# A two-layer decoder trunk on one Trainium2 core: late stores on GpSimd's queue, the gate row written between the layers, biases in four transfers, score-bank fill on ScalarE, and the scale columns spread anew

## The chip, the cores and the metric

The kernel runs on one core of one Trainium2 chip (trn2). A core has five engines with a queue of instructions each: TensorE (PE in the profile; PEld is its weight load), VectorE (DVE), ScalarE (ACT), GpSimd (POOL) and SyncE (SP), which issues transfers. Every engine works through its queue in order, and waits on semaphores where it needs what another one makes. Transfers can be issued from SP, ACT and POOL, and run on 16 DMA engines.

The metric is the device time of one execution in microseconds (us), as the median of a few runs. A profiled execution has its own time, and a span from its first to its last instruction.

## The reference, cut to what matters

A sequence of 1024 rows of width 1024 goes through two layers. Layer 0 is a gated pooling mixer of width 2048; layer 1 is gated sliding-window attention (window 128, 16 query heads in 4 groups that the kernel takes one after another, 2 shared key/value heads) with a sink per head and a relative-position bias. Before each sub-layer stands RMSNorm with a shift and a scale worked out from a condition vector c, and behind it a gate from c.

```python
for l in range(DEPTH):                       # DEPTH = 2
    shift, scale, gate = split(silu(c) @ ada_w[l] + ada_b[l], 3)
    if l == 0:
        h = rmsnorm(x, norm_g[0]) * (1 + scale) + shift
        u, z = split(h @ w_in, 2)
        p = causal_multiscale_pool(u)        # trailing means over 2, 4, 8, 16 rows, minus u
        y = (einsum(p, w_group) * a_scale * silu(z)) @ w_out
    else:
        # one K/V from x, with its own norm, shift and scale
        kb, vb = shared_kv_blocks(x, silu(c), kv_norm_g, kv_ada_w, kv_ada_b, w_kv)
        h = rmsnorm(x, norm_g[1]) * (1 + scale) + shift
        q, z = split(h @ w_in, 2)
        s = q @ kb.T / 8 + pos_bias          # masked to the band of 128
        p = exp(s - m) / (sum(exp(s - m)) + exp(sink - m))
        y = ((p @ vb) * silu(z)) @ w_out
    x = x + gate * y
return rmsnorm(x, final_g)
```

## The kernel before, in words

**Tiling.** x is held transposed, as 8 tiles of 128 channels by 1024 rows, each worked on in two halves of 512 rows. Every fp32 operand is split into a high and a low part (`wh`, `wl` for a weight: ACT copies the high part, DVE subtracts for the low one), and each product is made of three matmuls: high by high, high by low, low by high. PE's order is that in which the code is written.

**Layer 0.** First the pooling stage (to about 420 us), then the output product in 16 *half products*: `order` lists pairs (n, hf) of an output tile n and a half hf of the 2048 inner channels; `out_half(i)` runs one. Tiles 0 to 4 (below `LATE = 5`) take both halves of the rows, 10.4 us each half product; tiles 5 to 7 take only the first half of the rows here and the second one in the next stage. The first six (`BESIDE = 6`) are written in a block in which only PE's order is by hand; in the ten that follow, all queues are in the order of the code.

**The scale columns.** The 64 columns of shift, scale and gate (48 for the two layers, 16 for K/V) are dot products, 128 at a time, of rows of `ada_w` and `kv_ada_w` with silu(c). 48 of them (`rest_cols`) are not wanted at once: for each, `ada_step` loads a 128x1024 tile into one of three `tmp` buffers from SP's queue, and one DVE instruction (`ada_dot`, L284) makes a column of `adac`. They are dealt out: 18 in the pooling stage, `ADA[i]` before the i-th of the first six half products, and the letters A in `JOBS` beside the last ten, where the load goes out from POOL's queue three jobs ahead (`ask`). A letter S there is another job: a weight of layer 1 is loaded, split and written back to DRAM (`stage_split`, `keep`). The last 8 columns are the gates of layer 1, `adac[:, 40:48]`.

**Between the layers** (about 556 to 605 us) a list of steps with times (`plan`, `at`) is sorted and written out for PE, ACT, DVE and POOL: the rest of the output product (`last_chunk`), the squares and the reciprocal root for the norm (`rstd_stats`), the modulation of two sets of eight tiles (`step_h`, `fold_l`), the loads of weights (`get_raw`) and their splits (`take_h`, `take_l`; L1057, L1061), and the shared K/V products. After it one transfer from ACT's queue loads the biases (L1105).

**Layer 1** is written as notes: each has an engine, a length, what it reads and writes. A planner (`in_order`) keeps PE's notes in their order and gives every other note a due time from those that need it; then it runs a clock over all queues, and takes on each the ready note that is due first. The lengths thus set only the order. `attend` is one block of 128 rows for four heads: scores into a bank of PSUM (`scores`), for block 0 with a memset of the missing part (L1413), then DVE takes the band out of it (L1422), adds the bias (L1429), ACT takes the exponential; the transposed probabilities are split, POOL selects parts of them (L1472) into `pp` and `ph`, two SP transfers copy half of `pp` to the other 64 partitions (L1483), and PE blends them with V (L1504, L1514). Weights of layer 1 that have been split once are kept in DRAM (`kw`), and fetched back from POOL's queue (L1758).

**The end.** For the last 128 rows, layer 1's gates and `final_g` are needed as rows: `rows_in` writes `adac[:, 40:48]` to DRAM as `row` from SP (L1635), and loads it and `fg_row` back to all partitions (L1641), the first after the write. `finish(0, 4, ...)` scales the first 512 rows and stores them, eight transfers of 256 KB from SP (`store`, L1858).

Of the kernel before, what the change touches and what calls it, by code (L numbers as in the profile page):

```python
# [18 lines left out]
P = 128  # L19
# [25 lines left out]

ADA = (0, 0, 2, 6, 8, 8)

BESIDE = 6

JOBS = ("S", "SA", "SA", "SA", "SA", "", "SA", "", "SA", "")  # L50

# [47 lines left out]
def trunk(ctx, tc, xT, c, pack, ada_first, ada_rest, wu0_in, wg0_in, wa, wg, wao, wkv,  # L99
# [48 lines left out]
    for i in range(16):  # L148
# [7 lines left out]
                            channel_multiplier=1, compare_op=ALU.is_ge, fill=0)  # L156

    early = cp.tile([P, 1], F32, name="early")
    nc.scalar.activation(early, ones, AF.Exp)
# [101 lines left out]
    with ExitStack() as sa:  # L261
# [610 lines left out]
        with tc.manual_schedule(engines={ET.PE}):  # L872
# [70 lines left out]
            def out_half(i):  # L943
# [7 lines left out]
                if hf == 1:  # L951
                    for q in qs:
                        residual(n, q, outs[n][q], 16)
                    for q in qs:
                        square_add(n, q)

            for i in range(BESIDE):
                ws[order[i + 1]] = half_w(*order[i + 1])
                if i == 0:
                    gather(8, 9)  # L960
                    new_x()
                    again_x(0)
# [9 lines left out]
        with tc.manual_schedule(engines={ET.PE, ET.Activation, ET.DVE, ET.Pool, ET.SP}):  # L972
            stage_hi = [slot("stage") for _ in range(2)]
            raw = fetch(wao[order[BESIDE + 1]])
            jobs, asked = list("".join(JOBS)), []
            for _ in range(3):
                ask()
            for i in range(BESIDE, len(order)):
                if i + 1 < len(order):
                    ws[order[i + 1]] = split_w(*raw)  # L980
                if i + 2 < len(order):
                    raw = fetch(wao[order[i + 2]])
                if i < KT:
# [5 lines left out]
            assert rest_at[0] == len(rest_cols) and not staged  # L989
            mod_scale(8, 56, C_KVG)  # L990
            mod_scale(16, 32, C_NG + 8)
# [84 lines left out]
        for i in range(nl):  # L1076
            at(NT * i, last_chunk, i)
            if i % 4 == 3:
                t, n = NT * (i + 1), late[i // 4]
                at(t + AFTER[0], lambda n: residual(n, 1, got[n], 16), n)  # L1080
                at(t + AFTER[1], square_s, n, 1)
                at(t + AFTER[2], square_a, n, 1)
        at(NT - 0.01, lambda: put("st", rstd_stats, sqh[0], 4))
        at(2 * NT - 0.01, lambda: nc.scalar.copy(out=rb, in_=rstd_spread(got["st"], 4)))
# [19 lines left out]
    bias = bp.tile([P, 16, P], F32, name="bias")  # L1104
    nc.scalar.dma_start(bias, bias_in)  # L1105
    KH = [bp.tile([P, T], F32R, name=f"KH{i}") for i in range(2)]
# [144 lines left out]
    X = [there(x) for x in xk]  # L1251
    KHb, KLb, VSb = [there(t) for t in KH], [there(t) for t in KL], there(VS)
    ring_of("wh", got["wv"][0], got["wq"][0])
    ring_of("wl", got["wv"][1], got["wq"][1])
# [136 lines left out]
    def attend(q, r, b):  # L1391
# [16 lines left out]
        def scores(j):  # L1408
# [3 lines left out]
            if b == 0:  # L1412
                note(DVE, 0.2, lambda: nc.vector.memset(s()[:, :, :P], NEG), (), [(bk, "off")])  # L1413

            def f():
                for e in range(2):
# [4 lines left out]
                 [(qt, (j, e, i, c)) for e in range(2) for i in range(2)] + k_on, [(bk, 0)])  # L1421
            note(DVE, 0.36, lambda: nc.vector.copy_predicated(  # L1422
                out=s()[:, :, :P], mask=tri, data=s()[:, :, P:]), [(bk, "off")], [(bk, 0)])
# [3 lines left out]
        def row(s, bk, e, i):  # L1427
# [38 lines left out]
        if b:  # L1466
# [4 lines left out]
            def some(to, h, sign, base):  # L1471
                note(POOL, 0.65, lambda: nc.gpsimd.affine_select(  # L1472
                    out=v8(to(), h), in_=v8(cur(), h).bitcast(F32),
                    pattern=[[0, 2], [0, 4], [-sign, 2], [-2 * sign, P // 4]], base=base,
                    channel_multiplier=sign, compare_op=ALU.is_ge, fill=0.0),
                    [(cur, (x, h)) for x in range(2)] if to is not cur else (),
                    [(to, (x, h)) for x in range(2)])
# [50 lines left out]
        def add(e):  # L1528
            es = slice(e * 2 * P, (e + 1) * 2 * P)
            note(DVE, 0.36, lambda: nc.vector.scalar_tensor_tensor(  # L1530
                out=of()[e * 64:(e + 1) * 64, :], in0=o()[0:64, es], scalar=0.5,
                in1=ol()[0:64, es], op0=ALU.mult, op1=ALU.add),
                [(o, 0), (o, 1), (ol, 0)], [(of, e)])
        for e in range(2):
            add(e)
        ofv = lambda: of().rearrange("p (j c) -> p j c", c=P)
        note(DVE, 0.5, lambda: nc.vector.tensor_mul(out=ofv(), in0=ofv(), in1=sz()[:, :, cols]),
             [(sz, 0), (sz, 1)], [(of, 0), (of, 1)])
# [36 lines left out]
    def out_part(q, part, n2):  # L1575

        def run(w):
            acts = heads(q, part, range(4))

            def tile(i, n):  # L1580
                def done(ps):
                    note(DVE, 0.68, lambda: residual(n, q, ps(), 40), [(ps, 0)], x_on(n, q))
                    if part == 1:
                        note_square(n, q)
# [46 lines left out]
    def rows_in():  # L1631

        row = kp.tile([KT, P], F32, name="row")
        at = there(row)
        note(SP, 0.35, lambda: nc.sync.dma_start(  # L1635
            row.rearrange("n p -> p n"), adac[:, 40:48]), last_w[3][0].on, [(at, 0)], 4.0)
# [131 lines left out]
    def split_any(key, raw, w):  # L1768
# [8 lines left out]
        else:  # L1777
# [3 lines left out]
        note(ACT, 1.0, lambda: nc.scalar.copy(out=w[0](), in_=raw()), [(raw, 0)], w[0].on)  # L1781
        note(DVE, 1.16, lambda: nc.vector.tensor_sub(
            out=w[1](), in0=raw(), in1=w[0]().bitcast(F32)), [(raw, 0)] + w[0].on, w[1].on)
# [45 lines left out]
    def finish(t0, n, gap):  # L1829
# [4 lines left out]
        def gen():  # L1834
# [46 lines left out]
    class Second:  # L1881
# [5 lines left out]
        def step(self, k):  # L1887
            if k % 2 == 0:
# [3 lines left out]
            b = adac[:, self.shift + k:self.shift + k + 1]  # L1892
            note(DVE, 0.77, lambda: nc.vector.scalar_tensor_tensor(
                out=f(), in0=xk[k][:, half(1)], scalar=a, in1=rb(), op0=ALU.mult, op1=ALU.mult),
# [172 lines left out]
```

## Time and profile before

| | |
|---|---|
| runs | 953.55, 954.9 and 952.06 us; median 953.55 |
| profiled execution | 956.07 us; its span 954.4 us |
| mean granted clock of TensorE | 0.989 |
| VectorE's work on the 48 scale columns | 60.7 us, and 37.6 us idle before them |
| DMA | 172.14 MB, 180 GB/s in the mean |

Of the profile's views, the list of waits tells for each engine what ended its idle time. A wait for several things is put down to the one that came last. In a group of instructions stand: line, engine, operation, out<-in, shapes, count, then busy us and mean ns of one, then idle us just before them with what ended it. A busy engine other than PE costs time only where PE waits for it.

### The profile page before, as it was taken

How to read it: one execution, taken by the hardware profiler on the slowest of the kernel's cores; microseconds unless marked ns; L12 is line 12 of the kernel's file. 1: busy time of each engine (PE TensorE's matmuls, PEld its weight loads, DVE VectorE, ACT ScalarE, POOL GpSimd, SP SyncE). 2: the span in 40 equal slices, each digit the busy share in tenths (PEclk: the TensorE clock that was granted, in tenths of full speed). 3: DMA queues.
4: the chain of work that ended last, by engine and by line, in shares of the span. 5: the costliest groups of instructions: out<-in, count | busy, mean ns of one | idle time of the engine just before them, and what ended most of it. 6: DMA issues, size and time to landing. Idle time of an engine off the chain costs nothing.

```text
span 954.4 us, 13163 instructions
## 1 busy us (share of the span) xinstructions
PE 917.1 (96%) x4532; PEld 800.4 (84%) x4532; DVE 761.8 (80%) x1382; ACT 493.0 (52%) x1000; POOL 175.4 (18%) x285
## 2 busy tenths in 40 slices
PE   8999899999999998999889999999999999998997
PEld 6887788888888887888778887788888888997887
DVE  6999989777997799786773759479999956776785
ACT  6546554433443354672122336377878656666544
POOL 3000000000000000000012200224324445545631
PEclk9999999999999999999999999999999999999999
DMA  9553441164216420778887933954776765567022
GB/s 342 185 181 111 141 168 66 52 236 155 67 50 237 154 67 23 264 229 308 289 290 272 324 117 132 346 164 156 251 259 214 236 189 184 161 206 180 18 101 89
DMA packets 61047, 172.14 MB, mean 180 GB/s; under 512 B 8498, under 2 KB 16818, under 8 KB 60851
## 3 DMA queue, kind: packets, MB, share of 16 engines
q1 hardware_dynamic: 48306, 125.14, 38.3%
q0 software_dynamic: 12240, 44.57, 14.3%
q10 hardware_dynamic: 432, 1.57, 0.5%
q8 instruction: 36, 0.59, 0.2%
q14 instruction: 33, 0.26, 0.1%
HBM read 129.04 MB, written 36.70 MB: 174 GB/s over the span
## 4 chain that ended last, share of the span: by engine, by line
PE 48%; DVE 30%; DMA 12%; issue 6%; ACT 4%; POOL 1%; DVEq 0%; ACTq 0%; POOLq 0%; SPq 0%
PE ps_d L1268 7%; PE ps_d L1266 7%; PE ps_d L1267 7%; PE ps_d L257 5%; DMA tmp<-ada_rest 5%; PE ps_d L695 4%; DVE tmp L593 4%; PE ps_S L257 4%; DVE ws L666 2%; PE ps_S L695 2%; PE ps_tp L257 2%; DVE ad L284 1%; DVE tw L670 1%; PE ps_tp L695 1%; DVE p L616 1%
## 5 line engine op out<-in xcount | busy, mean ns | idle before, releaser
L284 DVE CUSTOM_DVE_ANT_0 tmp<-tmp,cact,pk 128x1024 f32<-128x1024 f32 x48 | 60.7, 1281 | 37.6 <-DMA tmp<-ada_rest 37.5
L257 PE MATMUL ps_d<-gh,wh 128*128 128x512 f32 x224 | 80.5, 383 | 0.0
L695 PE MATMUL ps_d<-hs,ws 128*128 128x512 f32 x312 | 72.1, 380 | 1.4 <-ACT ws L665 1.0
L1433 ACT ACTIVATE P<-P,nm 128x129 f32<-128x129 f32 x128 | 50.2, 394 | 34.9 <-DVE nm L1429 34.5
L1266 PE MATMUL ps_d<-hm,wh 128*128 128x512 f32 x176 | 67.9, 386 | 0.0
L695 PEld LDWEIGHTS ps_d<-hs,ws 128*128 128x128 f32 x312 | 58.8, 189 | 10.7 <-ACT ws L665 1.4
L1268 PE MATMUL ps_d<-hm,wl 128*128 128x512 f32 x176 | 66.8, 379 | 0.0
L1267 PE MATMUL ps_d<-hm,wh 128*128 128x512 f32 x176 | 66.8, 379 | 0.0
L257 PE MATMUL ps_S<-gh,wh 128*128 128x512 f32 x192 | 65.2, 380 | 0.0
L665 ACT CAST ws<-tw 128x512 fp32r<-128x512 f32 x52 | 31.8, 620 | 59.9 <-DVE tw L670 30.7
L1472 POOL TENSOR_SCALAR_AFFINE_SELECT pp<-ph 128x512 fp32r<-128x512 f32 x56 | 48.5, 883 | 72.4 <-DVE ph L1462 31.7
L585 POOL MEMSET tmp<- 128x16 f32 x12 | 1.3, 111 | 327.1 <-DVE tmp L593 112.3
L695 PE MATMUL ps_d<-ha,ws 128*128 128x512 f32 x252 | 57.8, 379 | 0.0
L695 PEld LDWEIGHTS ps_d<-ha,ws 128*128 128x128 f32 x252 | 47.7, 189 | 6.7
L257 PEld LDWEIGHTS ps_d<-gh,wh 128*128 128x128 f32 x224 | 42.7, 191 | 6.1
L1472 POOL TENSOR_SCALAR_AFFINE_SELECT ph<-ph 128x512 fp32r<-128x512 f32 x56 | 46.3, 843 | 0.0
L593 DVE TENSOR_TENSOR tmp<-tmp 128x1039 f32<-128x1039 f32 (+3 forms) x36 | 44.4, 1233 | 1.0
L257 PE MATMUL ps_d<-gh,wl 128*128 128x512 f32 x112 | 42.8, 382 | 0.0
L1444 ACT ACTIVATE P<-P,den 128x128 f32<-128x128 f32 x128 | 40.6, 390 | 3.1 <-DVE den L1440 3.1
L257 PEld LDWEIGHTS ps_S<-gh,wh 128*128 128x128 f32 x192 | 36.2, 189 | 4.9
L170 ACT CAST wh<-raw 128x1024 fp32r<-128x1024 f32 x24 | 25.2, 1049 | 27.7 <-PE ps_d L257 24.0
L257 PE MATMUL ps_d<-p,wh 128*128 128x512 f32 x96 | 36.6, 381 | 2.4 <-ACT p L615 1.7
(350 smaller groups left out, 2684.3 us busy)
## 6 DMA issues: line engine op xcount, KB each, us to landing
tmp<-ada_rest SPq DMA_DIRECT2D x42, 512.0 KB, 4.8
raw<-wa SPq DMA_DIRECT2D x28, 512.0 KB, 3.3
raw<-wao SPq DMA_DIRECT2D x20, 512.0 KB, 5.8
raw<-kw POOLq DMA_DIRECT2D x20, 512.0 KB, 4.6
wh<-kw POOLq DMA_DIRECT2D x19, 512.0 KB, 3.6
wl<-kw POOLq DMA_DIRECT2D x19, 512.0 KB, 4.8
ad<-ada_first SPq DMA_DIRECT2D x16, 512.0 KB, 4.5
x<-xT SPq DMA_DIRECT2D x32, 256.0 KB, 5.8
```

Of the source, the lines that this page charges most:

```text
L170: nc.scalar.copy(out=wh, in_=raw)
L257: mm(p, lhs, acts(k, hl, q), start=start and k == ks[0] and s == 0, stop=stop and k == ks[-1] and s == 2)
L284: nc.vector.tensor_tensor_reduce(out=raw, in0=raw, in1=ca, scale=0.5, scalar=pk[:, bcol:bcol + 1], op0=ALU.mult, op1=ALU.add, accum_out=ad ...
L593: nc.vector.tensor_add(out=nx[:, 2 * s - 1:], in0=cur[:, 2 * s - 1:], in1=cur[:, s - 1:PAD + T - s])
L665: nc.scalar.copy(out=ws[i][:, 0, :], in_=src)
L695: mm(ps, lhs, acts(k, hl), start=start and k == 0 and s == 0, stop=k == 3 and s == 2, skip_group_check=True)
L1266: mm(p, lh, a[0](), start=k == 0, stop=False)
L1267: mm(p, lh, a[1](), start=False, stop=False)
L1268: mm(p, ll, a[0](), start=False, stop=k == n - 1)
L1433: note(ACT, 0.41, lambda: nc.scalar.activation(pt()[:, i, :P + 1], pt()[:, i, :P + 1], AF.Exp, bias=nm()[:, i:i + 1], scale=-1.0, accum_ou ...
L1444: note(ACT, 0.3, lambda: nc.scalar.activation(pt()[:, i, :P], pt()[:, i, :P], AF.Copy, scale=den()[:, i:i + 1]), [(den, i)], [(pt, i)])
L1472: note(POOL, 0.65, lambda: nc.gpsimd.affine_select(out=v8(to(), h), in_=v8(cur(), h).bitcast(F32), pattern=[[0, 2], [0, 4], [-sign, 2], [- ...
```

## The change

- `ADA` falls from 24 to 16 columns, and `JOBS` gets three more A, in the iterations that had no job. The five columns that are left (`n_late`) are put into the plan between the layers, at 0.4, 1.9, 3.4, 4.9 and 6.4 us of its time, and their loads go out from SP.
- Beside the first half products the next half weight is fetched one iteration ahead (`fetch`, then `split_w`).
- The write of `row` moves from the end into the plan between the layers, at 9.0, on ACT's queue. The loads of the two rows go from SP to ACT, both after the split of the last weights; the first no longer follows the write.
- The biases are loaded in four transfers of four heads each from SP, as notes, and the step that adds the bias reads its own part.
- The score bank's memset on DVE becomes a copy on ACT from a constant tile `off`, which POOL fills at the start.
- The eight stores of the first 512 rows go from SP to POOL.
- Lengths of some notes are raised (DVE's, and POOL's selects from 0.65 to 0.85).

```diff
-ADA = (0, 0, 2, 6, 8, 8)
+ADA = (0, 0, 2, 4, 5, 5)
...
-JOBS = ("S", "SA", "SA", "SA", "SA", "", "SA", "", "SA", "")
+JOBS = ("S", "SA", "SA", "SA", "SA", "A", "SA", "A", "SA", "A")
...
+    off = cp.tile([P, P], F32, name="off")
+    nc.gpsimd.memset(off, NEG)
...
+            raw = fetch(wao[order[1]])
             for i in range(BESIDE):
-                ws[order[i + 1]] = half_w(*order[i + 1])
+                ws[order[i + 1]] = split_w(*raw)
+                raw = fetch(wao[order[i + 2]])
...
-            raw = fetch(wao[order[BESIDE + 1]])
             jobs, asked = list("".join(JOBS)), []
...
+        row = kp.tile([KT, P], F32, name="row")
+        n_late = len(rest_cols) - rest_at[0]
+        for i in range(n_late):
+            at(0.4 + 1.5 * i, ada_step)
+        at(9.0, lambda: nc.scalar.dma_start(row.rearrange("n p -> p n"), adac[:, 40:48]))
         at(NT - 0.01, lambda: put("st", rstd_stats, sqh[0], 4))
...
-    nc.scalar.dma_start(bias, bias_in)
...
+    biasb = there(bias)
...
-                note(DVE, 0.2, lambda: nc.vector.memset(s()[:, :, :P], NEG), (), [(bk, "off")])
+                note(ACT, 0.36, lambda: nc.scalar.copy(
+                    out=s()[:, :, :P], in_=off.unsqueeze(1).broadcast_to([P, 2, P])),
+                    (), [(bk, "off")])
...
-            note(DVE, 0.36, lambda: nc.vector.copy_predicated(
+            note(DVE, 0.4, lambda: nc.vector.copy_predicated(
...
-                accum_out=nm()[:, i:i + 1]), [(bk, 0)], [(pt, i), (nm, i)])
+                accum_out=nm()[:, i:i + 1]), [(bk, 0), (biasb, hd // 4)], [(pt, i), (nm, i)])
...
-                note(POOL, 0.65, lambda: nc.gpsimd.affine_select(
+                note(POOL, 0.85, lambda: nc.gpsimd.affine_select(
...
     def rows_in():
 
-        row = kp.tile([KT, P], F32, name="row")
-        at = there(row)
-        note(SP, 0.35, lambda: nc.sync.dma_start(
-            row.rearrange("n p -> p n"), adac[:, 40:48]), last_w[3][0].on, [(at, 0)], 4.0)
         rows = (row.rearrange("n p -> (n p)").unsqueeze(0), fg_row)
 
-        def load(name, src, on):
+        def load(name, src):
             t = end[name] = tile_of("raw1", bp, [P, 1024], F32, 2)
-            note(SP, 0.35, lambda: nc.sync.dma_start(t(), src.broadcast_to([P, D])),
-                 on, [(t, 0)], 4.0)
-        load("gate", rows[0], [(at, 0)])
-        load("gain", rows[1], ())
+            note(ACT, 0.35, lambda: nc.scalar.dma_start(t(), src.broadcast_to([P, D])),
+                 last_w[3][0].on, [(t, 0)], 4.0)
+        load("gate", rows[0])
+        load("gain", rows[1])
...
             def store(k):
-                note(SP, 0.35, lambda: nc.sync.dma_start(outT[k * P:(k + 1) * P, ts], xk[k][:, ts]),
+                on, by = (POOL, nc.gpsimd) if n == 4 else (SP, nc.sync)
+                note(on, 0.55 if n == 4 else 0.35,
+                     lambda: by.dma_start(outT[k * P:(k + 1) * P, ts], xk[k][:, ts]),
                      x_of(k), (), 3.0)
...
+    def bias_part(r):
+        hs = slice(4 * r, 4 * r + 4)
+        note(SP, 0.35, lambda: nc.sync.dma_start(bias[:, hs], bias_in[:, hs]),
+             (), [(biasb, r)], 5.0)
+    for r in range(4):
+        bias_part(r)
```

The other lengths that change: the two additions of `add(e)` from 0.36 to 0.4, the gating product from 0.5 to 0.58, the residual from 0.68 to 0.72, the low part of a weight from 1.16 to 1.22, and the modulation's first step from 0.77 to 0.85.

More of the change, by code (lines that the diff above doesn't have):

```diff
@@ L988, in trunk @@
                 out_half(i)
-            assert rest_at[0] == len(rest_cols) and not staged
+            assert not staged
             mod_scale(8, 56, C_KVG)
@@ L1529, in add @@
             es = slice(e * 2 * P, (e + 1) * 2 * P)
-            note(DVE, 0.36, lambda: nc.vector.scalar_tensor_tensor(
+            note(DVE, 0.4, lambda: nc.vector.scalar_tensor_tensor(
                 out=of()[e * 64:(e + 1) * 64, :], in0=o()[0:64, es], scalar=0.5,
@@ L1536, in attend @@
         ofv = lambda: of().rearrange("p (j c) -> p j c", c=P)
-        note(DVE, 0.5, lambda: nc.vector.tensor_mul(out=ofv(), in0=ofv(), in1=sz()[:, :, cols]),
+        note(DVE, 0.58, lambda: nc.vector.tensor_mul(out=ofv(), in0=ofv(), in1=sz()[:, :, cols]),
              [(sz, 0), (sz, 1)], [(of, 0), (of, 1)])
@@ L1581, in done @@
                 def done(ps):
-                    note(DVE, 0.68, lambda: residual(n, q, ps(), 40), [(ps, 0)], x_on(n, q))
+                    note(DVE, 0.72, lambda: residual(n, q, ps(), 40), [(ps, 0)], x_on(n, q))
                     if part == 1:
@@ L1781, in split_any @@
         note(ACT, 1.0, lambda: nc.scalar.copy(out=w[0](), in_=raw()), [(raw, 0)], w[0].on)
-        note(DVE, 1.16, lambda: nc.vector.tensor_sub(
+        note(DVE, 1.22, lambda: nc.vector.tensor_sub(
             out=w[1](), in0=raw(), in1=w[0]().bitcast(F32)), [(raw, 0)] + w[0].on, w[1].on)
@@ L1892, in step @@
             b = adac[:, self.shift + k:self.shift + k + 1]
-            note(DVE, 0.77, lambda: nc.vector.scalar_tensor_tensor(
+            note(DVE, 0.85, lambda: nc.vector.scalar_tensor_tensor(
                 out=f(), in0=xk[k][:, half(1)], scalar=a, in1=rb(), op0=ALU.mult, op1=ALU.mult),
```

## The prediction

> **What bounds the kernel now.** I read the share of busy time by engine first, then the list of TensorE's (PE's) waits, then the stretches in which the longest waits lie (busy time, granted clock and DMA by stretch), and last the rows of the engine or queue that each wait names.
>
> ```profile
> PE 917.1 (96%) x4532; PEld 800.4 (84%) x4532; DVE 761.8 (80%) x1382; ACT 493.0 (52%) x1000; POOL 175.4 (18%) x285
> ```
>
> PE is busy for 917.1 of 954.4 us. Its order of work is fixed and the change adds no matmul, so what the change can win is a part of the 37.3 us in which PE stands, and what the clock loses after a stop. Here are PE's waits that the edits touch (total in us, times, longest):
>
> ```profile
> PE ps_o L1514 <- DMA pp<-pp: 4.5, 1, 4.5
> PE ps_o L257 <- DVE wl L172: 2.9, 2, 2.0
> PE ps_tp L257 <- DVE wl L172: 2.4, 2, 1.7
> PE ps_S L1418 <- DVE ps_S L1413: 2.2, 1, 2.2
> PE ps_d L1268 <- DMA raw<-kw: 1.7, 1, 1.7
> PE ps_d L246 <- DVE wl L1061: 1.1, 2, 0.6
> PE ps_o L1504 <- POOL ph L1472: 0.9, 2, 0.5
> ```
>
> And the stretches around them (length; busy time of each engine; then granted clock, DMA share, GB/s):
>
> ```profile
> core 0: us, PE busy (x) PEld busy (x) DVE busy (x) ACT busy (x) POOL busy (x), PEclk, DMA share, GB/s
> 481.50:487.00 5.50, 5.50 (x18) 4.54 (x19) 3.64 (x6) 0.00 (x0) 0.00 (x0) 0.69 0.90 311
> 564.10:602.00 37.90, 36.18 (x163) 30.26 (x162) 36.17 (x47) 23.50 (x26) 0.65 (x2) 1.00 0.40 141
> 692.70:698.50 5.80, 5.74 (x26) 5.16 (x27) 5.33 (x18) 4.72 (x16) 1.39 (x3) 0.71 0.83 272
> 864.40:874.00 9.60, 9.60 (x59) 8.71 (x58) 8.98 (x22) 6.31 (x19) 5.66 (x8) 1.00 0.47 33
> 874.00:882.00 8.00, 3.53 (x16) 3.09 (x15) 2.29 (x11) 2.44 (x10) 1.67 (x2) 0.78 1.06 355
> 882.00:888.00 6.00, 6.00 (x22) 4.91 (x22) 3.64 (x6) 2.89 (x8) 3.94 (x5) 0.72 0.13 40
> ```
>
> The reader is to see three things. A stop of PE of 2 us or more is paid twice: the stretch behind the 2.0 us stop has a clock of 0.69, which loses 5.5 x 0.31 = 1.7 us; behind the 2.2 us stop 5.8 x 0.29 = 1.7; around the 4.5 us stop 8 x 0.22 + 6 x 0.28 = 3.4. Between 564 and 602 us, which is the stretch between the layers, VectorE (DVE) is busy for 36.2 of 37.9 us and so has no room. And from 864.4 to 874 us the DMA engines are 0.47 busy but move only 33 GB/s.
>
> **The change, part by part.** *Scale columns before the layers' seam.* Each of the 48 columns is a load and one DVE instruction (L284). 24 of them lie in the six half products after the pooling stage (434 to 493 us):
>
> ```profile
> L284 DVE CUSTOM_DVE_ANT_0 tmp<-tmp,cact,pk 128x1024 f32<-128x1024 f32 x24 | 30.3, 1282 | 20.2 <-DMA tmp<-ada_rest 20.1
> L172 DVE TENSOR_TENSOR wl<-raw,wh 128x1024 fp32r<-128x1024 f32 x4 | 4.9, 1218 | 0.0
> ```
>
> DVE spends 30.3 us on them and 20.2 us standing before them for their loads, and the weight splits (L172), which PE waits for, stand behind them in DVE's order. That is 50.5 us for 24, or 2.1 us each. With 16 in their place DVE gets 8 x 2.1 = 17 us free in this stretch, against four waits of 2.9 + 2.4 = 5.3 us in all. So I take all of the 5.3 away, and the 1.7 us of clock behind the longest: 7.0 (bounds 3.5 and 7.0). That the half weights are asked for one earlier adds nothing by itself: DVE had 0.0 idle before L172, so their loads were not late. Three of the eight go to GpSimd's (POOL's) queue, into a stage for which the list of waits names nothing; they could bring back there what left here, so between 0 and 5.3; I take 0.5, nearer to the row that is absent.
>
> *Five columns between the layers.* They come ahead of the modulation of layer 1 in DVE's order, and the rest of DVE's work is queued behind them.
>
> ```profile
> 558.54 0.24 DVE L303 SCALAR_TENSOR_TENSOR acol<-adac,pk 128x8 f32<-128x8 f32 x2
> 559.86 0.16 DVE L208 TENSOR_SCALAR v<-ps_o 128x4 f32<-128x4 f32 x1 [1.08 <-PE ps_o L205]
> 564.11 0.75 DVE L1017 SCALAR_TENSOR_TENSOR tmp<-x,acol,rb 128x512 f32<-128x512 f32 x1 [4.09 <-ACT rb L1084]
> ...
> L284 DVE CUSTOM_DVE_ANT_0 tmp<-tmp,cact,pk 128x1024 f32<-128x1024 f32 x48 | 60.7, 1281 | 37.6 <-DMA tmp<-ada_rest 37.5
> ```
>
> Five times 60.7 / 48 = 1.26 is 6.3 us; DVE's idle time here is 1.08 + 4.09 = 5.2, so at best 1.1 us is left over, less 0.5 for two memsets of 0.27 that leave DVE (row below). But there are three buffers, and a load takes 4.8 us to land (row below): if the first column ends at 560.0, the fourth lands at 564.8, and the fifth ends near 567.4 instead of 564.1. From there to 602 DVE is full and PE already waits for its splits (L246, 1.1), so most of it reaches PE. If all five loads are late, it is 7. I take 3.0 (bounds 0.6 and 7).
>
> *The row of gates.* The trace shows what its write does:
>
> ```profile
> 862.04 0.58 SPq L1635 DMA_DIRECT2D row<-adac  x1
> 868.67 2.13 SPq L1483 DMA_DIRECT2D pp<-pp  x2
> ...
> tmp<-ada_rest SPq DMA_DIRECT2D x42, 512.0 KB, 4.8
> raw<-wao SPq DMA_DIRECT2D x20, 512.0 KB, 5.8
> pp<-pp SPq DMA_DIRECT2D x56, 64.0 KB, 1.9
> out<-x SPq DMA_DIRECT2D x8, 256.0 KB, 2.2
> bias<-bias_in ACTq DMA_DIRECT2D x1, 1024.0 KB, 9.1
> raw<-row SPq DMA_DIRECT2D x1, 512.0 KB, 8.8
> row<-adac SPq DMA_DIRECT2D x1, 4.0 KB, 11.7
> ...
> 868.67 11.52 DMA pp<-pp
> ```
>
> 4 KB, in pieces of 4 bytes, take 11.7 us from 862.04 to 873.7, which is the stretch at 33 GB/s; the copy of pp behind it takes 11.52 us (last row, from the chain of waits) instead of 1.9, and PE waits for it. With the write gone from here, the 4.5 and the 3.4 us go: 7.9 (bounds 4.5 and 7.9). Next late is the copy at its usual 1.9 us: it would land at 870.6, and PE came to it at 880.2 - 4.5 = 875.7. The write is now issued by ScalarE (ACT) between the layers, and drains there for 9.6 us. What it meets there are the loads of wao, and after them those of the K/V weights:
>
> ```profile
> 566.31 5.73 SPq L179 DMA_DIRECT2D raw<-wao  x2
> 576.12 1.03 ACT L1057 CAST wh<-raw 128x1024 fp32r<-128x1024 f32 x1
> ```
>
> The first is asked for at 566.31 and split from 576.12, 9.8 us later; it needs 5.8, so 4.0 are in hand. Caught whole by the drain it is 9.6 - 4.0 = 5.6 late, with 3.4 of clock behind it: bounds 0 and 9.0. I take 1.0, since it goes out before DVE has done the first tile's modulation, behind which ACT issues the write. The two broadcast loads of rows now go out from ACT when the last weights are split, without waiting for the write; ACT's exponentials stand behind the two issues. 0.
>
> *The score bank.* Eight memsets of 0.27 us leave DVE for ACT. One is late:
>
> ```profile
> 691.07 1.23 DVE L1782 TENSOR_TENSOR wl<-raw,wh 128x1024 fp32r<-128x1024 f32 x1
> 692.35 0.27 DVE L1413 MEMSET ps_S<- 128x256 f32 x1
> ```
>
> It stands behind a weight split, and costs PE 2.2 + 1.7 = 3.9. ACT is only 52% busy over the span, but busy in 4.72 of the 5.80 us after 692.7, so a fill there can be late as well: bounds 0 and 3.9, and I take 3.0.
>
> The Trainium skill (TensorE: Matmul & The Clock Gate, Part 1: The HAM clock gate) has the clock halved after an idle window of about 3.4 us. By that, stops of 2.0 and 2.2 us cost no clock, and their two 1.7 us are not there to win: 943.1 in the end (rival 5). The rows of 0.69 and 0.71 behind just these stops disagree, and I go by them.
>
> *The biases.* One transfer of 1 MB on ACT's queue (9.1 us) becomes four on SyncE's (SP's), with the same bytes. PE's 1.7 us wait for a kept weight at 609 us falls into it. The four parts start a little later, and only the first is wanted soon; the scores of each head group now wait for their part. Bounds -1.7 (the same wait once more) and 1.7; I take 1.0 off.
>
> *The stores.* Eight stores go from SP to POOL, whose instructions of this kind are
>
> ```profile
> L1758 POOL DMA_DIRECT2D raw<-kw x20 | 10.9, 544 | 54.5 <-DVE wl L1061 40.2 <-PE ps_d L1268 14.1
> L1472 POOL TENSOR_SCALAR_AFFINE_SELECT pp<-ph 128x512 fp32r<-128x512 f32 x4 | 3.5, 886 | 6.5 <-PE ps_o L1514 6.5
> ```
>
> 0.54 us each, 4.3 us in all, and the selects (second row, between 908 and 929 us), for which PE already waits 0.9, stand behind each store that waits for its row. 0 to 4.3; I take 0.5, since POOL is idle for 6.5 us before four of them. The new lengths in the planner only shift its order: 0, +-2.
>
> **Sum**: 7.0 + 7.9 + 3.0 + 1.0 = 18.9 off, and 0.5 + 3.0 + 1.0 + 0.5 = 5.0 on: 13.9 off. The profiled execution took 956.07 us with a span of 954.4; the median is 953.55. The terms are differences, so they are taken from the median: 939.7.
>
> **The rivals.**
> 1. *The stops are moved, not removed.* The loads of the columns stay late in both later places: the 3 + 5 columns cost 5.3 + 7 instead of 3.5. For it: 20.2 us of DVE waiting for such loads in the row above. Against: the DMA engines have room there (0.40). 953.55 - 18.9 + 13.8 = 948.5.
> 2. *The write clogs the seam*, and the kernel is slower. If the write goes out ahead of the load that is wanted next, the drain holds that load and the one behind it, which lands 9.6 + 5.8 + 5.8 = 21.2 us after its issue and is 11.4 late. PE stops for that and loses 3.4 of clock; DVE, in whose order the split stands, stops as long, and having 1.7 us of slack hands 9.7 on to the splits for K and V, which PE waits for again. At worst 953.55 - 18.9 + 4.0 + 11.4 + 3.4 + 9.7 = 963.2; it is slower than before from a loss of 14.9 us here, and with half of it 950.9. Against: the 4.0 us in hand, and the share of 0.40.
> 3. *The write wasn't it* (the change doesn't do what it says): the slow stretch belongs to the POOL loads of the same time and stays. 939.7 + 7.9 = 947.6. Against: 33 GB/s isn't a full queue.
> 4. *Stores hold the selects*: a select behind a store that waits for its row of x, 4.3 + 1.7 of clock: 939.7 - 0.5 + 6.0 = 945.2. Against: POOL's 6.5 idle us, and stores whose rows come late in DVE's order anyway. The Trainium skill (DMA: Bandwidth & Descriptors, Issuing engine by pattern) gives plain loads and stores to SyncE and calls that path generally faster, which speaks against this edit; no run here has shown these stores from POOL yet.
> 5. *Short stops don't lower the clock*; the slow clock of 482 and 693 us has another reason and stays: 939.7 + 1.7 + 1.7 = 943.1. Against: it follows both stops at once.
>
> **Chances.** The forecast 0.55 (its own range 935 to 944), rivals in order 0.18, 0.07, 0.05, 0.08, 0.07. From the best bound of every term (7.0 + 7.9 + 3.9 + 1.7 off, 0.6 on: 933.6) to rival 1 and a little above it, the range is 934 to 950; beyond lie rival 2 and the ends. A difference of 0.3% (2.9 us) is about what a measurement of this kernel can tell from none. Faster: all but most of rival 2 and a part of the worst of rival 1, 0.89; same 0.05; slower 0.06.
>
> **What would show it.** In the profile after: no wait of PE for L172 splits before 490 us; no 11 us row write near 862 and none of PE's waits for pp; a row write between 565 and 575 us with 30 to 40 GB/s behind it; L1413's wait gone. PE's waits between 556 and 605 us tell the price of the five columns: 2 more is right, 5 or more is rival 1, a weight load of over 15 us there is rival 2. A wait of PE over 2 us for a select after 900 us is rival 4. If the time is right but the 864 us stretch still stands, it is right for the wrong reason.

## The result, and the profile after

The changed kernel takes 949.29 us (median of 9 runs, 946.27 to 951.11), the kernel before 955.49 us in the 9 runs beside them. The ratio is 0.9935, with a 95% interval of 0.9917 to 0.9954: 6.2 us faster, 4.4 to 7.9 by the interval. Forecast were 939.7 and a gain of 13.9 us. The profiled execution took 947.24 us, its span 945.5 us (before: 956.07 and 954.4).

First the busy time of the engines in the changed kernel, then its list of PE's waits (total in us, times, longest); the lines have moved by 2 or 3, and by 8 to 10 in the last stages.

```profile
PE 913.9 (97%) x4532; PEld 797.8 (84%) x4532; DVE 759.6 (80%) x1374; ACT 494.9 (52%) x1008; POOL 181.7 (19%) x297
```

```profile
PE ps_o L207 <- DVE sqh L238: 6.1, 1, 6.1
...
PE ps_d L248 <- DVE wl L1064: 1.1, 2, 0.6
...
PE ps_tp L259 <- DVE wl L174: 1.1, 1, 1.1
...
PE ps_o L1514 <- POOL ph L1482: 0.9, 2, 0.5
```

Most of what was to go is gone: the waits for L172's splits (now L174) fell from 5.3 to 1.1 us, and those for the copy of pp (4.5), the score bank (2.2) and the kept weight at 609 us (1.7) are no longer in the list. A new one stands at its head: 6.1 us for the sum of squares, at the seam between the layers. Its stretches, and three in which the old waits lay (length; busy time of each engine; then granted clock, DMA share, GB/s):

```profile
482.00:500.00 18.00, 18.00 (x85) 15.77 (x84) 6.04 (x8) 3.65 (x5) 3.14 (x6) 1.00 0.75 259
...
690.00:698.00 8.00, 8.00 (x48) 7.25 (x47) 7.91 (x22) 7.51 (x22) 2.74 (x4) 1.00 0.88 292
864.00:874.00 10.00, 10.00 (x59) 9.02 (x59) 9.31 (x27) 7.15 (x25) 6.37 (x8) 1.00 0.74 254
```

```profile
552.03:558.08 6.05, 0.00 (x1) 0.00 (x0) 3.81 (x8) 0.63 (x1) 0.00 (x0) 0.72 0.59 205
558.08:565.10 7.02, 7.01 (x21) 5.97 (x22) 2.72 (x7) 0.00 (x0) 2.05 (x1) 0.51 0.27 103
```

In the three old places the clock is at 1.00, and the stretch near 864 us moves 254 GB/s instead of 33. At the seam PE stands for 6.05 us, and then works 7.02 us at a clock of 0.51, which loses 3.4 more: 9.5 us. VectorE's (DVE's) order there shows why, with SyncE's (SP's) row of the five loads put in by time (start, length; idle time before it and what ended it in brackets):

```profile
546.86 1.28 DVE L286 CUSTOM_DVE_ANT_0 tmp<-tmp,cact,pk 128x1024 f32<-128x1024 f32 x1
546.97 14.79 SPq L300 DMA_DIRECT2D tmp<-ada_rest  x5
...
554.27 1.28 DVE L286 CUSTOM_DVE_ANT_0 tmp<-tmp,cact,pk 128x1024 f32<-128x1024 f32 x1 [6.12 <-DMA tmp<-ada_rest]
...
555.48 0.75 DVE L747 SCALAR_TENSOR_TENSOR x<-ps_tp,adac,x 128x512 f32<-128x512 f32 x1
556.15 1.27 DVE L286 CUSTOM_DVE_ANT_0 tmp<-tmp,cact,pk 128x1024 f32<-128x1024 f32 x1
...
557.35 0.69 DVE L238 TENSOR_TENSOR sqh<-sqh,sq 128x512 f32<-128x512 f32 x1
```

The dot product at 554.27 is the first of the five late columns. DVE waits 6.12 us for its load, which SP could issue only at 546.97, when the dot that began at 545.66 had ended and freed a `tmp` buffer. Behind it in DVE's order stand the residual of the last half product (L747), a second late column, and the last addition of squares (L238), which PE's statistics wait for. PE had ended that half product by 549.5 us.

The two profiles add up. Gone are 4.2 + 1.7 us (early splits and clock), 4.5 + 2.5 (copy of pp), 2.2 + 1.7 (score bank) and 1.7 (kept weight), 18.5 in all; come are 9.5 at that stop and 0.5 of other waits at the seam. That leaves 8.5, where the two profiled executions differ by 8.8; the medians, over more runs, differ by 6.2.

### The profile page after: what moved, and what is told of

Read it like the earlier page. It is cut to its first block, busy times and chain, and to the rows that moved or that the text cites. A ratio compares the mean times of both kernels' runs of the same rounds, so it can differ in the third digit from the quotient of the medians.

```text
span 945.5 us, 13153 instructions
## 1 busy us (share of the span) xinstructions
PE 913.9 (97%) x4532; PEld 797.8 (84%) x4532; DVE 759.6 (80%) x1374; ACT 494.9 (52%) x1008; POOL 181.7 (19%) x297
## 5 line engine op out<-in xcount | busy, mean ns | idle before, releaser
L259 PE MATMUL ps_S<-gh,wh 128*128 128x512 f32 x192 | 67.1, 391 | 0.0
L172 ACT CAST wh<-raw 128x1024 fp32r<-128x1024 f32 x24 | 25.2, 1050 | 36.1 <-PE ps_d L259 28.7
L174 DVE TENSOR_TENSOR wl<-raw,wh 128x1024 fp32r<-128x1024 f32 x24 | 29.3, 1222 | 12.9 <-ACT wh L172 12.0
```

The source lines that it names most:

```text
L174: nc.vector.tensor_sub(out=wl, in0=raw, in1=wh.bitcast(F32))
L259: mm(p, lhs, acts(k, hl, q), start=start and k == ks[0] and s == 0, stop=stop and k == ks[-1] and s == 2)
```

## The experiments

Every time is a median, and each ratio compares with the kernel before, run beside it on the same chip. Differences between two runs are given by the medians; by the ratios they come out up to 1.3 us larger or smaller.

| run | edit against | us | ratio to before (95%) |
|---|---|---|---|
| late in jobs | changed kernel | 955.83 | 1.0001 (0.9976 to 1.0026) |
| late behind v | changed kernel | 943.62 | 0.9872 (0.9840 to 0.9904) |
| old columns | changed kernel | 945.19 | 0.9894 (0.9862 to 0.9926) |
| row at end | changed kernel | 953.94 | 0.9974 (0.9951 to 0.9997) |
| row later | late behind v | 951.82 | 0.9966 (0.9947 to 0.9985) |
| bank on DVE | row later | 954.72 | 0.9999 (0.9980 to 1.0018) |
| stores on SP | row later | 951.58 | 0.9967 (0.9949 to 0.9985) |
| row alone, at 34 | before | 957.74 | 1.0027 (1.0003 to 1.0051) |
| row in gap | late behind v | 950.66 | 0.9957 (0.9934 to 0.9980) |
| bank on DVE 2 | row in gap | 954.17 | 1.0007 (0.9984 to 1.0030) |
| row alone, at 25.5 | before | 955.33 | 1.0012 (0.9987 to 1.0038) |
| three behind v | changed kernel | 941.82 | 0.9853 (0.9817 to 0.9889) |
| row alone, at 9 | before | 952.30 | 0.9974 (0.9952 to 0.9997) |
| three, bank on DVE | three behind v | 946.84 | 0.9913 (0.9883 to 0.9943) |
| three, two in jobs | changed kernel | 950.51 | 0.9943 (0.9921 to 0.9965) |
| row in 32 bytes | row in gap | 942.18 | 0.9867 (0.9838 to 0.9895) |

**Where the late columns stand.** Theory: the loss is DVE's order at the seam. Rivals: the row's write, or the columns wherever they are. The expectations count the half clock as 5.1 us; but PE stood through 6.05 x 0.28 / 0.50 = 3.4 of its 10.24 us, so 3.4 is the loss.

*Late in jobs:*

```diff
-JOBS = ("S", "SA", "SA", "SA", "SA", "A", "SA", "A", "SA", "A")
+JOBS = ("SA", "SA", "SA", "SA", "SA", "AA", "SA", "AA", "SAA", "AA")
```

> No column between the layers: the five go to the ten half products before them (14 columns there instead of 9), all else as in the changed kernel. Theory (what is missing is the stop at 552 us, 6.05 us, and the 10.24 us at half clock behind it, 5.1 us, both made by the first late column's load, for which DVE stands in front of the last half product's residual): both go, 949.3 - 11.2 = 938.1, with no wait of PE over 1 us between 493 and 600 us. Rival (the row write or the new order of the plan costs it): the stop at the seam stays, 947 to 950. Rival (a column costs 2.1 us wherever it stands, since the DMA engines are 0.82 busy there already): waits of PE for L174 or L259's weights between 493 and 552 us, 942 to 949.

The theory missed this by 18 us. The waits say where:

```profile
PE ps_o L207 <- DVE sqh L238: 5.1, 1, 5.1
PE ps_tp L259 <- ACT wh L172: 2.1, 1, 2.1
PE ps_d L259 <- ACT wh L172: 2.1, 1, 2.1
```

The stop at the squares is still there, with no column between the layers at all: in the last job a dot now waits 4.57 us for its load, ahead of the same residual. Two half weights are late before it, which is the sign of the second rival; but DVE's rows show the same order there too:

```profile
548.87 1.28 DVE L286 CUSTOM_DVE_ANT_0 tmp<-tmp,cact,pk 128x1024 f32<-128x1024 f32 x1 [5.78 <-DMA tmp<-ada_rest]
...
550.08 0.74 DVE L747 SCALAR_TENSOR_TENSOR x<-ps_d,adac,x 128x512 f32<-128x512 f32 x1
```

A dot waits 5.78 us for its load in front of an earlier residual. ScalarE (ACT) squares what that residual writes, and has the copy of the half weight (L172) behind the square in its own order; PE waits for the copy. At 533.60 it is the same, with 5.22 us. So it isn't the plan that matters, but a column whose load is late, in front of a residual.

*Late behind v:*

```diff
-            at(0.4 + 1.5 * i, ada_step)
+            at((2.7, 2.8, 2.9, 3.0, 3.1)[i], ada_step)
```

> The same five columns stay between the layers, but all five stand behind the statistics' v in DVE's order (plan times 2.7 to 3.1 instead of 0.4 to 6.4), and no more ahead of the last residual and the squares. Theory (order): the stop at 552 us and its half clock go; five dots of 1.26 us stand in 4.2 us of idle time, so the first modulation is 2 to 3 us later: 938.1 + 2.5 = 940.6. Rival (amount: five loads of 512 KB and 6.3 us of DVE cost what they cost there): 947 to 950, with the same time lost to PE's waits elsewhere between 552 and 603 us.

943.62 us: 5.7 under the changed kernel, with the same columns and the same loads. (v, L210, is DVE's first step after the sum of squares.) The wait at the squares is gone, and another one has come:

```profile
PE ps_S L259 <- ACT wh L1060: 3.4, 1, 3.4
```

DVE's timeline shows the order now:

```profile
548.89 0.75 DVE L747 SCALAR_TENSOR_TENSOR x<-ps_tp,adac,x 128x512 f32<-128x512 f32 x1 [1.98 <-PE ps_tp L259]
...
552.27 0.16 DVE L210 TENSOR_SCALAR v<-ps_o 128x4 f32<-128x4 f32 x1 [1.08 <-PE ps_o L207]
...
559.35 1.28 DVE L286 CUSTOM_DVE_ANT_0 tmp<-tmp,cact,pk 128x1024 f32<-128x1024 f32 x1 [1.05 <-DMA tmp<-ada_rest]
...
560.56 0.75 DVE L1020 SCALAR_TENSOR_TENSOR tmp<-x,acol,rb 128x512 f32<-128x512 f32 x1
561.23 1.22 DVE L1064 TENSOR_TENSOR wl<-raw,wh 128x1024 fp32r<-128x1024 f32 x1
```

The residual waits for PE alone. The split L1064 now ends 10.2 us behind v; only then is the next half of wao asked for (562.47), 0.7 us ahead of the row's write. It lands 12.7 us later, and PE stands for it.

*Old columns:*

```diff
-ADA = (0, 0, 2, 4, 5, 5)
+ADA = (0, 0, 2, 6, 8, 8)
...
-JOBS = ("S", "SA", "SA", "SA", "SA", "A", "SA", "A", "SA", "A")
+JOBS = ("S", "SA", "SA", "SA", "SA", "", "SA", "", "SA", "")
```

> The changed kernel with the columns spread as before (24 and 6, none between the layers); row write, biases, score bank and stores as changed. Theory: the early waits of 4.2 us and 1.7 us of clock come back and the seam's 11.2 us go: 949.3 + 5.9 - 11.2 = 944.0. Rival (the row write clogs the seam, the columns have no part in it): the stop at the seam stays and the early ones come on top, 955. Rival (the early stops were worth nothing since PE caught up later): 938 to 940.

945.19, by the theory. No wait at the seam is over 0.6 us, although the row's write stands where the change put it; the early waits are back in full:

```profile
PE ps_o L259 <- DVE wl L174: 4.6, 2, 2.6
PE ps_tp L259 <- DVE wl L174: 1.7, 2, 1.2
```

By the medians, everything but the new spread of the columns is thus worth more than the change as a whole.

**What the row's write is worth.** *Row at end* (the row written and loaded on SP's queue in `rows_in`, as before the change):

```diff
-        at(9.0, lambda: nc.scalar.dma_start(row.rearrange("n p -> p n"), adac[:, 40:48]))
...
+        note(SP, 0.35, lambda: nc.sync.dma_start(
+            row.rearrange("n p -> p n"), adac[:, 40:48]), last_w[3][0].on, [(at, 0)], 4.0)
```

> The changed kernel with the row of gates written and loaded on SP's queue in the last stage, as before. Theory (the write holds the copy of pp behind it): PE's wait of 4.5 us for pp and 3.4 us of clock come back, and 0.6 us at the seam go: 949.3 + 7.3 = 956.6. Rival (the write wasn't the cause, or the stop is taken by something else by now): 949, the copy of pp landing in 2 to 5 us beside the write.

953.94, 4.7 more than the changed kernel instead of 7.3 (3.7 by the ratios). The wait is back, a little shorter:

```profile
PE ps_o L1522 <- DMA pp<-pp: 4.3, 3, 3.8
```

The 4.7 is a net. In this trace the end costs 4.3 of waiting and 1.7 of clock (3.41 us at half), 6.0 in all; but the stop at the seam is cheaper than in the changed kernel, 5.5 and 2.4 of clock instead of 6.1 and 3.4. Why the seam differs is not shown.

*Row later* (late behind v, and):

```diff
-        at(9.0, lambda: nc.scalar.dma_start(row.rearrange("n p -> p n"), adac[:, 40:48]))
+        at(34.0, lambda: nc.scalar.dma_start(row.rearrange("n p -> p n"), adac[:, 40:48]))
```

> As the run with the five columns behind v, and the row of gates written at plan time 34 instead of 9, when the last half weights (wq's) have been asked for and nothing is wanted from the DMA queues for 10 us. Theory (with the columns out of the way the write is the next late thing: a load of wao took 12.7 us beside it, and PE stood 3.4 us for it with 1.7 us of clock): 943.6 - 5.1 = 938.5, no wait of PE over 1.5 us between 493 and 600 us. Rival (that load is late because DVE asked for it late, behind the five dots): the wait of 3.4 us stays, 942 to 944. Rival (the write clogs the loads of the kept weights and the biases in its new place): a wait of 2 us or more between 595 and 625 us, 942 or more.

951.82: the 3.4 us are gone, and the last rival came in their place. The kept weights and the biases are asked for within 10 us of the write.

```profile
PE ps_d L1276 <- DMA raw<-kw: 5.6, 1, 5.6
```

*Row in gap* (the same line at plan time 25.5):

> As the run with the five columns behind v, with the row of gates written at plan time 25.5 (about 585 us), when the load of wv has just landed and the next load (wq's, asked for near 589 us) is not split before 596 us. Theory (the write holds up every load asked for within 10 us of it, wherever it stands; it costs nothing where none of these is wanted soon): neither the wait of 3.4 us near 573 (row at 9) nor those of 6.3 us near 607 (row at 34), 943.6 - 5.1 = 938.5, waits of PE over 1.5 us between 493 and 625 us: none. Rival (the five columns make the loads late, the write only stands beside it): 942 to 944 with a wait of 3 us near 573. Rival (the write costs about 5 us wherever it stands between the layers): 943 or more, with a wait of 2 us or more between 590 and 610 us.

950.66; the theory that the write is free there fell too. The write goes out at 585.33, wb's load at 589.00, with the write still under way. Issues to landing between 580 and 605 us (KB each, median us):

```profile
raw<-wb SPq DMA_DIRECT2D x1, 512.0 KB, 14.2
...
row<-adac ACTq DMA_DIRECT2D x1, 4.0 KB, 12.8
```

PE stood 4.7 us for that load, and the last rival is the nearest: with five columns behind v the write cost 3.4, 4.7 and 6.3 us of waiting at its three places, each time at another load. Why it is so dear the next run shows. *Row in 32 bytes*, against the row in the gap (it leaves out the right order of the gates in the row, so what it shows is the traffic alone):

```diff
-row.rearrange("n p -> p n"), adac[:, 40:48]
+row.rearrange("n p -> (n p)").rearrange("(p n) -> p n", n=KT), adac[:, 40:48]
```

> The run with the row at plan time 25.5, where the write took 12.8 us and PE stood 4.7 us, with the same 4 KB written in 128 pieces of 32 bytes instead of 1024 of 4 (the gates then lie in another order in the row, so the last gating multiplies by the wrong gates: the order of the row is the part of the computation that is changed). Theory (the number of pieces holds the DMA engines): the write lands in 2 to 4 us, wb's load in 4 to 5 us instead of 14, PE's wait of 4.7 us near 600 and its half clock go: 950.7 - 4.7 - 3.4 = 942.6 or a little less. Rival (any write from ScalarE's queue at that place holds the loads): 950 to 951, wb's load still at over 10 us.

942.18, 8.5 us less, and the same list reads

```profile
raw<-wb SPq DMA_DIRECT2D x3, 512.0 KB, 10.6
...
row<-adac ACTq DMA_DIRECT2D x1, 4.0 KB, 1.4
```

(the first row is now a median with two later loads; this one took 4.1). The bytes, the queue and the place are the same; the 1024 pieces of 4 bytes made the 12.8 us. The Trainium skill (DMA: Bandwidth & Descriptors, Specifications) puts the least size for full rate at 512 bytes, with a read-modify-write below it, and under "Why small descriptors are slow" a fixed cost for each packet. The two runs agree that pieces count and not bytes, 12.8 us against 1.4; they can't tell the two mechanisms apart, since pieces of 32 bytes lie below that size too.

*Row alone* was tried at three plan times in the kernel before: 34, 25.5 and 9, with the two loads on ScalarE.

> The kernel before with one edit: the row of gates written from ScalarE between the layers (plan time 34, all its columns being there by then) and its two broadcast loads from ScalarE. The prediction's term: 4.5 us of waiting and 3.4 us of clock go, 955.0 - 7.9 = 947.1. By the run with the row at the end of the changed kernel (4.6 us slower than the changed kernel): 955.0 - 4.7 = 950.3. Rival (the write costs as much in the new place): 955.

> The kernel before with the row of gates alone moved, to plan time 25.5, and its two loads on ScalarE's queue. The prediction's term: 955.5 - 7.9 = 947.6, the waits before 500 us and near 690 us as before. By the run with the row at the end of the changed kernel: 955.5 - 4.7 = 950.8. Rival (it costs as much in the new place): 955.

> The kernel before with the row of gates alone moved, at the changed kernel's own plan time 9, its two loads on ScalarE's queue. At plan times 34 and 25.5 the new place cost 8.4 and 4.9 us of waiting and as much as the old one in all. If the place at 9 is free when no late column stands in the way: the end's 4.5 us of waiting and 3.4 us of clock go, 955 - 7.9 = 947.1 (the prediction's term), or 950.3 by the 4.7 us which the row at the end cost the changed kernel. Rival (it costs as much here too): 955.

At 34 it is slower by 0.03 to 0.51%, at 25.5 no different, at 9 faster by 2.9 us (0.3 to 4.6 by the interval). In all three the wait for pp is gone (0.3 us is left in the second), so the end was freed each time; PE stood 8.4 and 4.9 us for kept weights and wq in the first two, and 0.6 us for a half of wao in the third.

**The other terms.** *Bank on DVE*, in three pairs (the fill by `nc.vector.memset` again):

> The run with the row later, and the score bank filled by VectorE's memset again, as before the change. Theory (the memset stands behind a weight split): PE's wait of 2.2 us near 680 us and 1.7 us of clock come back, 938.5 + 3.9 = 942.4. Rival (that wait came from where the stage stood in time, not from the engine): 938 to 939.

> The run with the row at 25.5, and the score bank filled by VectorE's memset as before the change. In the earlier pair, both with the stop of 6 to 8 us near 607, the memset's wait did not come back. Theory of the prediction (the memset stands behind a weight split, wherever the stage begins): a wait of 2.2 us near 680 us and 1.7 us of clock, 938.5 + 3.9 = 942.4. Rival (that wait hangs on where the planner sets the fill): no such wait, 938 to 939.5.

> The run with three columns behind v, and the score bank filled by VectorE's memset. Theory of the prediction: a wait of 2.2 us at the memset's tile near 680 us and 1.7 us of clock, 3.9 us slower than its pair. Rival (in the changed kernel's order the fill isn't late on either engine): no such wait, within 1 us of its pair.

2.9, 3.5 and 5.0 us slower than their pairs (3.2, 4.8 and 5.7 by the ratios): about the size forecast. But no wait of 2.2 us came back. What all three traces have and none of their pairs has is 1.7 us of waits in layer 1: one of 0.5 for a memset, and 1.2 in short ones between 735 and 780 us for other work of DVE and the copies of pp. The rest of each difference is open. In the last pair it is partly 1.5 us more waiting at the seam, which lies ahead of the first memset (590 us) and so can't come from it. In the first pair 2.2 us of it are a longer wait for a kept weight.

*Stores on SP:*

```diff
-                on, by = (POOL, nc.gpsimd) if n == 4 else (SP, nc.sync)
-                note(on, 0.55 if n == 4 else 0.35,
+                on, by = SP, nc.sync
+                note(on, 0.35,
...
```

> The run with the row later, and the eight late stores on SP's queue again. Theory (POOL's stores are hidden): the same time within 1 us, 938.5. Rival (stores before selects cost POOL's queue): 1 to 6 us faster. Rival (SP's queue was the limit for the copies of pp there): slower by 1 to 4 us, with a wait of PE for pp.

951.58 against 951.82: no difference. PE's wait for POOL's selects is 0.9 us in both.

**A version that beats both.** *Three behind v:*

```diff
-ADA = (0, 0, 2, 4, 5, 5)
+ADA = (0, 0, 2, 4, 6, 6)
...
-            at(0.4 + 1.5 * i, ada_step)
+            at((2.7, 2.8, 2.9)[i], ada_step)
```

> The changed kernel with three late columns instead of five, all behind v in DVE's order, the other two in the last two of the six half products (18 there instead of 16); the row of gates at plan time 9 as in the changed kernel. Theory (the row's write costs nothing if the load of wao ahead of it is asked for 6.5 us behind v, as in the run with the old columns, and 3.4 us if 10.2 us behind, as with five dots in between; three dots of 1.26 us fit into 4.1 us of idle time): no wait of PE over 1 us between 493 and 625 us, waits of 1 to 2 us near 467 and 479, 938 to 941. Rival (the write costs 3 us or more at the seam with any late column): a wait of 2 us or more near 575, 942 or more.

941.82 us, 13.4 less than before: close to the 13.9 forecast for the change, but with another spread of the columns. Its longest waits behind 440 us:

```profile
PE ps_o L259 <- DVE wl L174: 2.0, 1, 2.0
PE ps_d L248 <- DVE wl L1064: 1.1, 2, 0.6
```

*Three, two in jobs* (ADA as changed, "AA" in the sixth and eighth job):

> As with three columns behind v, but the other two go to the ten half products before the seam (11 there instead of 9, 16 in the six before). Theory: the early waits stay at 1 us, and 11 columns fit where 14 did not (waits of 2.1 and 2.1 us, and the last residual held for 5.1): 937 to 940. Rival (that stage's DMA queues are full at 9): a wait of 1 to 5 us between 530 and 560 us, 942 to 950.

950.51, with the wait that the rival named:

```profile
PE ps_tp L259 <- ACT wh L172: 4.4, 1, 4.4
```

The trace shows no fuller queues (a DMA share of 0.77 over 493 to 545 us, against 0.79 with three behind v), but the order that late in jobs showed:

```profile
549.72 1.29 DVE L286 CUSTOM_DVE_ANT_0 tmp<-tmp,cact,pk 128x1024 f32<-128x1024 f32 x1 [6.37 <-DMA tmp<-ada_rest]
...
550.93 0.75 DVE L747 SCALAR_TENSOR_TENSOR x<-ps_d,adac,x 128x512 f32<-128x512 f32 x1
551.71 0.63 ACT L234 ACTIVATE sq<-x 128x512 f32<-128x512 f32 x1 [12.41 <-DVE x L747]
552.25 1.03 ACT L172 CAST wh<-raw 128x1024 fp32r<-128x1024 f32 x1
```

The load of this dot went out at 541.41, when the dot before it had freed a buffer, and took 8.2 us (how much of that is other traffic is open); the residual, its square and the copy of the half weight stand behind it.

## Why the prediction was wrong, point by point

The direction was right and 949.3 lies in the range, but the gain is less than half of the forecast. The step that failed is "Five columns between the layers": "They come ahead of the modulation of layer 1 in DVE's order", "I take 3.0 (bounds 0.6 and 7)". It let DVE's work behind v pay, 6.3 us of dots against 5.2 of idle time. The first two columns in fact came ahead of the last residual and the squares, which is ahead of v, and DVE stood there for a load that couldn't go out before a buffer was free; the prediction had counted the three buffers, but as free for the first three loads. The term measured 9.5, above its upper bound, which had no clock in it. Putting 9.5 in place of 3.0 makes 7.4 out of the 13.9, inside the measured 4.4 to 7.9. That the other terms fit is in part luck: the row's term was too large, and the score bank's came by another path.

- *Columns before the seam, 7.0*: 5.9 between the two profiles, within its bounds, and the waits come back with the old columns. Right.
- *The row's write leaves the end, 7.9*: the wait and the slow stretch at 33 GB/s went, but the size was too large. By the runs it is 4.7 (row at end, 6.0 in its trace without the cheaper seam) and 2.9 (row alone, at 9). Of the 3.4 us of clock 0.9 had been counted while PE stood: the kernel before, by stretch,

```profile
875.85:880.32 4.47, 0.00 (x1) 0.03 (x1) 0.45 (x2) 0.42 (x3) 0.00 (x0) 0.80 1.08 367
880.32:885.40 5.08, 5.08 (x14) 4.26 (x15) 2.01 (x5) 2.82 (x7) 3.79 (x5) 0.50 0.45 163
```

  loses 5.08 x 0.50 = 2.5. The stop itself was 3.8 us in the run that brought it back, and the half clock behind it 3.4 us long instead of 6.8. Part of what the row alone gives is lost again elsewhere in its trace: 3.4 us of waits for weights at the seam instead of 1.6, and 6.9 us of early ones instead of 5.3.
- *Row write at the seam, 1.0 (0 to 9.0)*: 0 in the changed kernel; the wait of 0.6 at 588 us stands in the run with the row at the end too. What decides is how long after the load of the half of wao, which goes out about 0.7 us ahead of the write, PE comes to that half. With late behind v this is 10.4 us, the load takes 12.7, and PE stands 3.4. In the changed kernel, with the old columns and with three behind v it is 11.6 to 12.5 us, the load takes 9.7 to 11.2, and PE doesn't stand for it. In the other places the write cost 4.7 to 8.4 us of waiting. Rival 2's mechanism is real, and the change was clear of it by 0.7 us: the copy of that half ended at 580.79, and PE came to it at 581.47.
- *Score bank, 3.0*: 2.9 to 5.0, of which the traces place 1.7; the one wait that the term was made of doesn't come back with the memset, so the size is luck. The 2.2 us stay in all three runs with the row alone, and are gone with the old columns, so neither of these edits took them away; the new lengths of the planner's notes could have, and no run tests that.
- *Stores, 0.5*: 0. *Three columns to JOBS, 0.5*: no wait there with 9. With 11 and 14 a dot's late load held a residual, and PE's waits for L172 came to 5.5 and 4.2 us, the same mechanism as at the seam.
- *Biases, 1.0*: the 1.7 us wait for the kept weight is gone. It is gone as well with the old columns, with the row at the end and with the memset on DVE, and it stands at 1.6 in the row alone at 9, so it was none of these edits. The biases, the earlier fetch and the new lengths weren't undone by themselves, so that the biases did it is only argued.
- *New lengths, 0*: no run takes them back alone, so what they did is open.
- *Rivals.* Rival 1 gave 948.5 and came nearest; its sign, 5 us or more between 556 and 605, came with one wait of 6.05 that begins at 552. Only its second place came true; with 9 columns the half products before the seam have no wait. Rivals 3 and 4 are out: the stretch at 864 us and the selects show it.
- *Rival 5* is out, since the clock is at 1.00 where the two short stops were; but not every short stop lowers it. A stop of 1.97 us in the version with three columns is followed by

```profile
481.30:486.30 5.00, 5.00 (x15) 4.10 (x16) 4.72 (x6) 1.97 (x3) 0.54 (x1) 0.66 0.80 243
```

  which loses 5.00 x 0.34 = 1.7 us; a longer one, of 2.7 us, in the row alone at 9 is not followed by one:

```profile
494.60:500.00 5.40, 5.40 (x25) 4.75 (x26) 5.24 (x6) 2.53 (x4) 0.95 (x2) 1.00 0.93 310
```

  The Trainium skill (TensorE: Matmul & The Clock Gate, Part 1: The HAM clock gate) has a window of 3413 ns that runs free of the kernel. The traces agree: but for the one that runs on to the end of each trace, every stretch at half clock is 3.41, 6.83 or 10.24 us long, and in the kernel before the four begin 132, 62 and 54 times 3.413 us apart. So where a stop falls counts beside its length. That the clock falls only after an idle window of 3.4 us is not what they show, and "a stop of 2 us or more is paid twice" isn't either: a stop of 1.3 us (three, bank on DVE, at 577.8) is followed by one.

## What to carry to other kernels

Work that is off the critical path still has a place in an in-order queue: before a filler with a load of its own is put there, ask what stands behind it, and when its load can go out at the earliest (here, when the filler before it has freed a buffer). A small transfer is priced by its pieces, and its price is paid by whatever is asked for from just ahead of it to some 10 us behind it; where that can't be nothing, make the pieces larger. A stop's second price, the half clock, counts only while PE works.

## What the runs showed of the hardware that was not expected

- 4 KB written in 1024 pieces of 4 bytes take 12.8 us and make a 512 KB load behind them take 14.2; in 128 pieces of 32 bytes they take 1.4, and the load 4.1.
- The half clock comes in multiples of 3.41 us, and one and the same stop can bring one or two of them: 3.41 us behind the 2.2 us stop for the memset in the kernel before, 6.83 behind it in the row alone at 9. It was 6.83 around the 4.5 us stop of the kernel before, and 10.24 around the 6.05 us of the changed kernel.
- The stage before the seam took 9 columns without a wait and 11 not, at a DMA share of 0.80 over 493 to 545 us with 9 (the changed kernel) and 0.77 with 11: the mean share said nothing of the limit, which showed as a load that went out only when a buffer came free.
